# Unscaled rows to DRAM, norm factors applied after the fetch, and another order for the last tile and the last down projection

## The chip, the cores and the metric

One Trainium2 chip, one of its cores. The metric is the device time of one execution in microseconds (us); the kernel before takes 776.83 us, the median of three runs (776.01 to 776.99). PE is TensorE, ACT is ScalarE, DVE is VectorE, POOL is GpSimd, SP is SyncE; "SPq" and "ACTq" in a row are DMA issues by those engines' sequencers.

## The reference

One decoder layer for 512 tokens of width 1024, in float32. A mixing part (gated convolution and differential attention) ends in an output projection that is added to the residual. Then a mixture of 32 SwiGLU experts in 4 groups; each token goes to the best group and there to its best two experts. The part that matters here:

```python
h = h + mix @ w_out
hn2 = rms_norm(h, ffn_norm_g)            # h * rsqrt(mean(h*h) + eps) * g
logits_g = hn2 @ w_router_group          # [T, 4]
logits_e = hn2 @ w_router_expert         # [T, 32]
g_idx, g_gate = argmax, max of softmax(logits_g)
top-2 of the 8 logits of that group, softmax over the two -> exp_w
comb = one_hot(g_idx) * exp_w * g_gate   # [T, 32], two entries of a row are not zero
for each expert e:
    act = silu(hn2 @ w_gate[e]) * (hn2 @ w_up[e]) * comb[:, e]
    y  += act @ w_down[e]
h = h + y
```

## The kernel before

The 512 tokens are four tiles of 128 (c = 0 to 3), and `y` in SBUF holds the residual, 128 x 4 x 1024. Each expert gets up to 64 slots, two experts make a pair (q = 0 to 15), so that a pair fills the 128 partitions. An overflow loop at the end takes experts with more than 64 tokens; in the run shown it takes no trip.

The weights of the experts, 192 pieces of 1 MB, come in through a ring of 16 tiles (`we`) and one more (`wm`), all issued by SP at L726 in the order in which PE uses them. SP issues a piece when the tile that it goes into has been read for the last time, and at most eight DMAs are under way on its and ACT's queues together: each takes one of eight semaphores in turn and waits until the DMA that had it before has landed. 12 pieces are issued while the output projection runs, five more (`pump(RING + MORE)`) as the tiles that hold the projection's operands come free.

Between the output projection and the first expert stands a handover, once per token tile c:

- `out_rest` (L829) is the rest of the projection, `h_add` (L665) adds its half to `y` on DVE and squares it on ACT, `h_transposed` (L675) turns `y` on PE, and `router` (L685) multiplies it with the router's weights.
- `h_norm` (L744) is a generator of small DVE and ACT steps that makes `rstd`. Its last step multiplies `y[:, c]` by `rstd` and by the norm's gain (`gfb`, loaded at L657) into the tile `ht`, of which there is one, in a transposed element order, and writes `ht` to DRAM as `hrow` (L763, 512 KB, issued by ACT).
- `route` (L781) picks group and experts in 14 small DVE steps. `tail` (L814) interleaves `h_norm` and `route`, and for tile c - 1 it is emitted around the projection of tile c. Engines run their queues in order.
- `positions` and `place` count the tokens of each expert. Once tile 3 is placed, `prepare` (L926) makes the list of a pair's tokens (`one_hot`, `index`), and POOL fetches their rows from `hrow` with an indirect DMA (`fetch_rows`, L917, tile `xr`), after all four writes of `hrow` have landed. `gates` (L862) makes the weights `comb`, written to DRAM as `crow` and fetched per slot as `cw`.

Per pair, `turned` (L938) turns the fetched rows with eight PE transposes and copies them out of PSUM, four by ACT in one instruction and four by DVE in one. `gate_up` (L951), `activate` (L958), `down_t` (L964), `down` (L972), `down_split` (L982) and `combine` (L995) follow. `down` of the last pair makes both halves of the 1024 columns together; then `combine` is called for eight blocks of `y`, each with its DVE add (L1003) and its DMA to the output (L1140).

Of the kernel before, what the change touches and what calls it, by code (L numbers as in the profile page):

```python
# [17 lines left out]
P = 128  # L18
D = 1024
# [14 lines left out]
NONE = 2047  # L34
PAIRS = NE // 2
# [3 lines left out]
def layer(ctx: ExitStack, tc: tile.TileContext, x, attn_norm_g, w_in, conv_w, conv_out_g,  # L39
# [101 lines left out]
    G.dma_start(gst[19:27], ffn_norm_g.rearrange("o (k p) -> (o k) p", p=P))  # L141
    lt = ring.tile([P, 2, 2, HD], F32, name="lt", tag="w")
# [513 lines left out]
    gfb = po.tile([P, D], F32, name="gfb")  # L656
    A.dma_start(gfb, bass.AP(tensor=ffn_norm_g.tensor, offset=ffn_norm_g.offset, ap=[[0, P], [1, D]]))  # L657
# [37 lines left out]
    comb = kp.tile([P, NT, NE], F32, name="comb")  # L695
# [16 lines left out]
    def w_src(e, j):  # L712
# [5 lines left out]
        src = src.rearrange("(p k) f -> p k f", k=4)  # L718
        return src[:, 2 * (j - 4):2 * (j - 4) + 2], (2, 1024)
# [19 lines left out]
    crow = dram.tile([S, NE], F32, name="crow")  # L739
# [4 lines left out]
    def h_norm(c):  # L744
# [91 lines left out]
    for c in range(NT):  # L836
# [17 lines left out]
    advance(tails[3], 50)  # L854
# [7 lines left out]
    def gates():  # L862
        eg4 = rtt("eg4", NT, NG)
# [11 lines left out]
        V.reciprocal(gate, gate)  # L875
        w12 = rtt("w12", 2, NT)
# [6 lines left out]
        V.tensor_add(comb, oh1, oh2)  # L883
# [26 lines left out]
    def fetch(i, m):  # L910
        x = moe.tile([P, KD, P], F32, name="xr", tag="xr", bufs=2)
        w = moe.tile([P, NE], F32, name="cw", tag="cw", bufs=4)
        fetch_rows(x, i, m)
        return x, w

    def fetch_rows(x, i, m):
        G.indirect_dma_start(out=x[0:m].rearrange("p k q -> p (k q)"), out_offset=None, in_=hrow[:, :],  # L917
# [40 lines left out]
    def activate(act, p, h, w):  # L958
        t = moe.tile([P, FE], F32, name="sil", tag="sil")
        A.activation(t[HS[h]], p[HS[1 - h]], AF.Silu)  # L960
# [20 lines left out]

    def down_split(p, m):  # L982
        rh = moe.tile([P, 2, 512], F32R, name="rh", tag="rh", bufs=2)
        rl = moe.tile([P, 2, 512], F32R, name="rl", tag="rl", bufs=2)
        for hf in range(2):
            A.activation(rh[0:m, hf], p[hf][0:m], AF.Copy)  # L986
            V.tensor_sub(rl[0:m, hf], p[hf][0:m], rh[0:m, hf].bitcast(F32))  # L987
        return rh, rl
# [6 lines left out]
    def combine(parts, m, c, hf):  # L995
# [7 lines left out]
        V.tensor_add(ys, ys, p)  # L1003
# [20 lines left out]
    def overflow(inc):  # L1024

        n = nc.values_load(tot[0:1, 0:1], min_val=0, max_val=NE)
        with tc.For_i(0, n, 1):
# [25 lines left out]
            V.tensor_mul(le[0:SLOTS], le[0:SLOTS], cw[0:SLOTS])  # L1053
# [5 lines left out]
            activate(act, p, 0, wcol[0:SLOTS])  # L1059
# [7 lines left out]
    for _ in range(2):  # L1067
        G.memset(moe.tile([P, KD, P], F32, name="xr", tag="xr", bufs=2), 0.0)
    for _ in range(4):
        G.memset(moe.tile([P, NE], F32, name="cw", tag="cw", bufs=4), 0.0)  # L1070
    ready = prepare((0, 1), "S")()
    gates()
    xts = {0: turned(rows.pop(0), P, "K")}
    ready()
# [19 lines left out]
    def expert(e):  # L1094
# [6 lines left out]
        activate(acts[q], p, h, cws[q][HS[h], e:e + 1])  # L1101
# [72 lines left out]
```

## Time and profile before

| what | before |
|---|---|
| median of three runs | 776.83 us |
| the profiled execution | 779.3 us |
| its span, first to last instruction | 777.5 us |
| mean granted clock of PE, share of 2.4 GHz | 0.965 |
| busy: PE, DVE, ACT, POOL | 692.2, 308.8, 179.3, 73.3 us |
| moved by DMA | 230.19 MB |
| chain that ended last | PE 49%, DMA 34%, DVE 9%, ACT 4% |

The page of the profile gives the busy time of each engine and the chain of work that ended last. The chain is followed back from the last instruction, at each step to what released it. Busy PE is pipelined work and not PE at its peak. The other views are windows (busy times, the granted clock and the rate of DMA in a stretch), the timeline and the list of waits.

### The profile page before, as it was taken

To read this page: it belongs to the slowest core of one execution; us is meant where nothing else is said; L and a number is where in the kernel's file an instruction comes from. 1 tells how busy PE (TensorE), PEld (TensorE's weight loads), DVE (VectorE), ACT (ScalarE), POOL (GpSimd) and SP (SyncE) were. 2 spreads that over 40 slices of the span, in tenths; PEclk is the share of its full clock that TensorE was granted. 3 is DMA by queue.
4 is the path that set the end of the run, shared out by engine and by line. 5 is a ranking of instruction groups with operands and counts; after the bars stand their busy time and mean duration, and the time that the engine had idled before them with its cause. 6 is when DMAs were issued, how large, how long until landed. Compare 5 with 4: busy or idle time off the path is not lost.

```text
span 777.5 us, 8615 instructions
## 1 busy us (share of the span) xinstructions
PE 692.2 (89%) x3272; PEld 375.5 (48%) x3272; DVE 308.8 (40%) x593; ACT 179.3 (23%) x363; POOL 73.3 (9%) x100
## 2 busy tenths in 40 slices
PE   6998999999999409899999999999988988998985
PEld 5887787777777303334334334334334333333431
DVE  3565776687442641143224133223223123211243
ACT  3555545545242111010110110110110110110010
POOL 5020301021100120202002002002002001000000
PEclk9999999999999758899999999999999999999998
DMA  8231221111279745999999999999999999999942
GB/s 256 84 91 52 75 82 55 55 54 63 73 268 422 295 156 233 415 420 421 417 420 420 418 421 414 423 420 415 422 421 419 418 421 421 416 421 421 422 190 108
DMA packets 53418, 230.19 MB, mean 296 GB/s; under 512 B 6287, under 2 KB 20896, under 8 KB 28800
## 3 DMA queue, kind: packets, MB, share of 16 engines
q1 hardware_dynamic: 48848, 222.32, 71.2%
q0 software_dynamic: 3280, 4.63, 1.9%
q10 hardware_dynamic: 1248, 2.69, 0.9%
q8 instruction: 26, 0.43, 0.2%
q14 instruction: 16, 0.13, 0.0%
HBM read 229.67 MB, written 4.26 MB: 301 GB/s over the span
## 4 chain that ended last, share of the span: by engine, by line
PE 49%; DMA 34%; DVE 9%; ACT 4%; issue 2%; POOL 1%; SPq 0%; ACTq 0%; POOLq 0%; DVEq 0%
DMA we<-in_w_exp_up_dram 23%; PE pgu L955 11%; PE pdn L978 7%; PE pgu L956 3%; PE pcb L1000 3%; DMA wm<-in_w_exp_down_dram 3%; PE pq L117 3%; DMA we<-in_w_exp_down_dram 3%; PE pq L116 3%; PE pq L118 3%; DMA hrow<-ht 3%; PE pcb L1001 3%; DMA xr<-hrow,idx 2%; PE pcv L116 1%; PE pcv L118 1%
## 5 line engine op out<-in xcount | busy, mean ns | idle before, releaser
L956 PE MATMUL pgu<-we,xt 128*64 128x512 f32 x488 | 217.9, 598 | 14.5 <-DMA we<-in_w_exp_up_dram 14.5
L955 PE MATMUL pgu<-we,xt 128*64 128x512 f32 x480 | 214.8, 598 | 0.8 <-issue 0.8
L961 DVE SCALAR_TENSOR_TENSOR act<-sil,cw,pgu 64x512 f32<-64x512 f32 x32 | 35.9, 1121 | 220.7 <-ACT sil L960 220.7
L978 PE MATMUL pdn<-we,aT 128*64 128x512 f32 x480 | 118.7, 606 | 1.5 <-ACT aT L969 1.5
L955 PEld LDWEIGHTS pgu<-we,xt 128*64 128x64 f32 x480 | 64.2, 138 | 87.9 <-issue 85.8
L956 PEld LDWEIGHTS pgu<-we,xt 128*64 128x64 f32 x488 | 65.3, 138 | 68.9 <-issue 41.9
L960 ACT ACTIVATE sil<-pgu 64x512 f32<-64x512 f32 x32 | 18.9, 591 | 291.5 <-PE pgu L956 266.4
L978 PEld LDWEIGHTS pdn<-we,aT 128*64 128x64 f32 x480 | 36.5, 139 | 67.2 <-issue 62.4
L1000 PE MATMUL pcb<-rh,sel 128*128 128x512 f32 x128 | 55.5, 434 | 7.0 <-DVE y L1003 6.7
L987 DVE TENSOR_TENSOR rl<-pdn,rh 128x512 fp32r<-128x512 f32 x32 | 22.1, 692 | 94.5 <-ACT rh L986 94.5
L1003 DVE TENSOR_TENSOR y<-y,pcb 128x512 f32<-128x512 f32 x72 | 48.6, 687 | 17.2 <-PE pcb L1001 16.5
L1001 PE MATMUL pcb<-rl,sel 128*128 128x512 f32 x128 | 51.3, 400 | 0.3
L917 POOL DMA_INDIRECT xr<-hrow,idx x16 | 16.1, 1005 | 362.3 <-DVE vcol L907 335.8
L108 DVE TENSOR_TENSOR wlo<-raw,whi 128x1024 fp32r<-128x1024 f32 x30 | 37.7, 1256 | 22.3 <-ACT whi L101 22.3
L986 ACT ACTIVATE rh<-pdn 128x512 fp32r<-128x512 f32 x32 | 19.1, 597 | 112.4 <-PE pdn L978 112.4
L116 PE MATMUL pq<-whi,xh 128*128 128x512 f32 x96 | 41.0, 427 | 2.4 <-DVE st0h L353 1.6
L116 PE MATMUL pcv<-xh,whi 128*128 128x512 f32 x96 | 41.7, 435 | 0.0
L117 PE MATMUL pq<-wlo,xh 128*128 128x512 f32 x96 | 38.8, 404 | 0.5 <-DVE wlo L108 0.5
L118 PE MATMUL pq<-whi,xl 128*128 128x512 f32 x96 | 38.7, 403 | 0.0
L118 PE MATMUL pcv<-xh,wlo 128*128 128x512 f32 x96 | 38.0, 395 | 0.0
L117 PE MATMUL pcv<-xl,whi 128*128 128x512 f32 x96 | 37.8, 394 | 0.0
L1000 PEld LDWEIGHTS pcb<-rh,sel 128*128 128x128 f32 x128 | 24.4, 191 | 26.3 <-DVE y L1003 20.2
(227 smaller groups left out, 907.8 us busy)
## 6 DMA issues: line engine op xcount, KB each, us to landing
we<-in_w_exp_up_dram SPq DMA_DIRECT2D x61, 1024.0 KB, 19.8
we<-in_w_exp_gate_dram SPq DMA_DIRECT2D x60, 1024.0 KB, 19.8
we<-in_w_exp_down_dram SPq DMA_DIRECT2D x60, 1024.0 KB, 19.8
raw<-in_w_in_dram SPq DMA_DIRECT2D x24, 512.0 KB, 3.7
raw<-in_w_out_dram SPq DMA_DIRECT2D x8, 512.0 KB, 3.7
wm<-in_w_exp_gate_dram SPq DMA_DIRECT2D x4, 1024.0 KB, 19.8
wm<-in_w_exp_down_dram SPq DMA_DIRECT2D x4, 1024.0 KB, 19.8
wm<-in_w_exp_up_dram SPq DMA_DIRECT2D x3, 1024.0 KB, 16.4
```

Source lines behind the costliest of these rows:

```text
L108: V.tensor_sub(los[i], raws.pop(i), his[i].bitcast(F32))
L116: T.matmul(o, lh, rh, start=start, stop=False)
L117: T.matmul(o, lh, rl, start=False, stop=False)
L118: T.matmul(o, ll, rh, start=False, stop=stop)
L955: T.matmul(p[HS[1 - h]], l, w[2 * (k // 4)][:, k % 4], start=(k == 0), stop=(k == KD - 1))
L956: T.matmul(p[HS[h]], l, w[2 * (k // 4) + 1][:, k % 4], start=(k == 0), stop=(k == KD - 1))
L961: V.scalar_tensor_tensor(act[HS[h]].rearrange("s (c q) -> s q c", c=4), t[HS[h]].rearrange("s (q c) -> s q c", c=4), w, p[HS[h]].rearrange ...
L978: T.matmul(p[hf][HS[h]], aT[:, c, HS[h]], ws2[h][c // 2][:, c % 2, hf * 512:(hf + 1) * 512], start=(c == 0), stop=(c == 3))
L987: V.tensor_sub(rl[0:m, hf], p[hf][0:m], rh[0:m, hf].bitcast(F32))
L1000: T.matmul(p, s[0:m, ts], rh[0:m, hf], start=(n == 0), stop=False)
L1001: T.matmul(p, s[0:m, ts], rl[0:m, hf], start=False, stop=(n == last))
L1003: V.tensor_add(ys, ys, p)
```

## The change

The rows written to DRAM are `y` itself, in its own element order, issued right after `h_transposed(c, 1)`; the tile `ht`, the gain `gfb` and the large multiplication of `h_norm` are gone. `rstd` becomes column 32 of `comb`, so that it comes back with the gates; `activate` applies it as the scale of the Silu and `gate` is multiplied by it once more. The gain, loaded at the start as `gf` (one column per turned block), is applied where `turned` copies out of PSUM: ACT does so in four instructions, one per block, DVE in one. For the last tile all 14 routing steps come first and the norm's steps move into `gates`. The first two pairs are prepared one after the other and not together. In the last pair the down weights come by columns, each half of the columns is finished and split by itself, the selection matrix is made ahead of `combine_all`, and of the four blocks of a half one is added by ACT (copy) and POOL (add) in place of DVE.

```diff
+    gf = cons.tile([P, KD], F32, name="gf")
+    G.dma_start(gf, ffn_norm_g.rearrange("o (p k) -> (o p) k", k=KD))
-    gfb = po.tile([P, D], F32, name="gfb")
-    A.dma_start(gfb, bass.AP(tensor=ffn_norm_g.tensor, offset=ffn_norm_g.offset, ap=[[0, P], [1, D]]))
@@ w_src
+        if isinstance(e, int) and e >= NE - 2:
+            return src[:, :, 512 * (j - 4):512 * (j - 4) + 512], (4, 512)
@@ h_norm
-        t = po.tile([P, KD, P], F32, name="ht")
-        V.scalar_tensor_tensor(t, y[:, c].rearrange("p (q k) -> p k q", k=KD), n,
-                               gfb.rearrange("p (q k) -> p k q", k=KD), op0=OP.mult, op1=OP.mult)
-        A.dma_start(hrow[c * P:(c + 1) * P, :], t.rearrange("p k q -> p (k q)"))
+        V.tensor_copy(comb[:, c, NE:NE + 1], n)
@@ tail
+        if c == NT - 1:
+            for g in (gr, gn):
+                for _ in g:
+                    yield
+            return
@@ the loop over c, and after it
         h_transposed(c, 1)
+        A.dma_start(hrow[c * P:(c + 1) * P, :], y[:, c])
-    advance(tails[3], 50)
+    advance(tails[3], N_ROUTE)
@@ gates
+        advance(tails[3], 50)
+        V.tensor_mul(gate, gate, rstd)
@@ turned
+        x = x.rearrange("s (q k) -> s k q", k=KD)
-                V.tensor_copy(xt[:, 4 * k2:4 * k2 + 4, 0:m], p[:, :, 0:m])
+                ks = slice(4 * k2, 4 * k2 + 4)
+                V.tensor_tensor(xt[:, ks, 0:m], p[:, :, 0:m], bc(gf[:, ks, None], [P, 4, m]), op=OP.mult)
-                A.activation(xt[:, 4 * k2:4 * k2 + 4, 0:m], p[:, :, 0:m], AF.Copy)
+                for j in range(4):
+                    A.activation(xt[:, j, 0:m], p[:, j, 0:m], AF.Copy, scale=gf[:, j:j + 1])
@@ activate
-        A.activation(t[HS[h]], p[HS[1 - h]], AF.Silu)
+        A.activation(t[HS[h]], p[HS[1 - h]], AF.Silu, scale=r)
@@ down_cols (new)
+        p = bank("D", "pdn")
+        for c in range(4):
+            for h in range(2):
+                T.matmul(p[HS[h]], aT[:, c, HS[h]], ws2[h][:, c], start=(c == 0), stop=(c == 3))
@@ combine
-        V.tensor_add(ys, ys, p)
+        if to is None:
+            V.tensor_add(ys, ys, p)
+        else:
+            A.activation(to, p, AF.Copy)
+            G.tensor_tensor(ys, ys, to, op=OP.add)
@@ before the first expert
-    ready = prepare((0, 1), "S")()
+    ready = [prepare((q,), "S")() for q in range(2)]
@@ the last pair
-    down_pair(q, down_t(acts.pop(q), P))
-    for c in range(NT):
-        for hf in range(2):
-            combine([parts[q]], P, c, hf)
+    sel = select(vcol[:, q:q + 1], P)
+    combine_all((q - 1,))
+    aT = down_t(acts.pop(q), P)
+    r = split_tiles()
+    yt = moe.tile([P, 2, 512], F32, name="yt", tag="xr", bufs=2)
+    pd = [down_cols([wt.pop((2 * q + h, 4 + hf)) for h in range(2)], aT) for hf in range(2)]
+    for hf in range(2):
+        split_half(r, pd[hf], hf, P)
+        for c in (0, 1, 2, 3):
+            combine([(sel, *r)], P, c, hf, yt[:, hf] if c == 1 else None)
             nc.sync.dma_start(oc[:, c, 512 * hf:512 * hf + 512], y[:, c, 512 * hf:512 * hf + 512])
```

## Rows read from the trace of the kernel before

**Rows 1.** Windows: busy us (instructions) by engine, granted clock, DMA share, GB/s.

```profile
core 0: us, PE busy (x) PEld busy (x) DVE busy (x) ACT busy (x) POOL busy (x), PEclk, DMA share, GB/s
...
240.00:260.00 20.00, 18.39 (x97) 13.80 (x96) 8.80 (x36) 4.76 (x13) 0.61 (x2) 1.00 1.01 422
260.00:280.00 20.00, 3.56 (x20) 3.15 (x21) 13.07 (x45) 2.13 (x7) 2.03 (x6) 0.56 0.49 174
280.00:300.00 20.00, 8.96 (x45) 4.58 (x46) 5.99 (x28) 2.19 (x4) 4.14 (x4) 0.59 0.38 116
...
500.00:600.00 100.00, 91.41 (x422) 37.63 (x420) 28.65 (x45) 10.98 (x19) 7.99 (x8) 1.00 1.01 420
```

**Rows 2.** Chain that ended last: start us, us, what (a DMA: issue to landing).

```profile
252.60 7.66 DMA hrow<-ht
...
270.79 6.93 DMA hrow<-ht
277.83 2.05 DVE ht L761
...
286.12 4.53 DMA xr<-hrow,idx
...
312.45 8.56 DMA xr<-hrow,idx
...
711.79 0.64 PE pgu L956
```

**Rows 3.** Timeline of the handover: start us, us, engine, line [idle before <-releaser].

```profile
253.61 0.40 PE L118 MATMUL po<-w1h,ml 128*128 128x512 f32 x1
...
255.25 0.68 DVE L667 TENSOR_TENSOR y<-y,po 128x512 f32<-128x512 f32 x1
...
265.11 0.68 DVE L667 TENSOR_TENSOR y<-y,po 128x512 f32<-128x512 f32 x1
...
267.64 1.92 PE L688 MATMUL pr<-wrg,hT 128*128 128x36 f32 x8 [0.63 <-ACT hT L683]
...
279.80 0.18 DVE L778 TENSOR_REDUCE rm<-w 128x1 f32<-128x32 f32 x1
...
281.77 0.19 DVE L812 SCALAR_TENSOR_TENSOR posm<-ppos,ohm 128x32 f32<-128x32 f32 x1 [0.28 <-PE ppos L809]
...
283.58 0.16 DVE L906 TENSOR_SCALAR idx<-pi 128x1 int32<-128x1 f32 x1 [0.36 <-PE pi L904]
...
286.12 1.12 POOL L917 DMA_INDIRECT xr<-hrow,idx  x1 [24.09 <-DVE oh L882]
...
293.65 1.08 PE L955 MATMUL pgu<-we,xt 128*64 128x512 f32 x1 [0.82 <-issue]
```

**Rows 4.** Timeline of SP's queue: the first piece issued into a freed tile.

```profile
298.71 0.33 SPq L726 DMA_DIRECT2D we<-in_w_exp_up_dram  x1
```

**Rows 5.** List of waits, 300 to 745 us: us in total, times, longest.

```profile
PE pgu L956 <- DMA we<-in_w_exp_up_dram: 14.5, 12, 1.3
```

**Rows 6.** Groups of ACT by shape: count, busy us, mean ns, idle before.

```profile
L948 ACT ACTIVATE xt<-pxt 128x512 f32<-128x512 f32 x16 | 9.5, 593 | 9.4 <-PE pxt L944 9.4
...
L596 ACT ACTIVATE so<-pav,hc 128x128 f32<-128x128 f32 x16 | 5.8, 362 | 4.9 <-PE pav L592 4.8
```

**Rows 7.** Router weights' tile: ns min/median/max, first to last start us.

```profile
L148 POOL DMA_DIRECT2D wr<-in_w_router_expert_dram x1: 889/889/889, 10.9 to 10.9; - x1
L285 DVE TENSOR_TENSOR wrg<-wr,gT x1: 458/458/458, 37.5 to 37.5; 128x288 f32<-128x288 f32 x1
```

**Rows 8.** Timeline of the last pair, columns as in Rows 3.

```profile
754.94 0.48 DVE L992 TENSOR_SCALAR sel<-tokrow,vcol 128x512 fp32r<-128x512 f32 x1
755.48 7.09 PE L978 MATMUL pdn<-we,aT 128*64 128x512 f32 x32 [0.75 <-ACT aT L969]
...
763.85 5.91 DVE L1003 TENSOR_TENSOR y<-y,pcb 128x512 f32<-128x512 f32 x8
```

**Rows 9.** Groups of POOL: count, busy us, mean ns, idle before.

```profile
L428 POOL TENSOR_TENSOR cs<-cs,cz 128x512 f32<-128x512 f32 x4 | 5.1, 1283 | 63.7 <-DVE cs L426 63.7
```

More of the change, by code (lines that the diff above doesn't have):

```diff
@@ L34 @@
 NONE = 2047
+N_ROUTE = 14
 PAIRS = NE // 2
@@ L694, in layer @@
     kp = ctx.enter_context(tc.tile_pool(name="kp", bufs=1, side="right", reuse_waits="tile"))
-    comb = kp.tile([P, NT, NE], F32, name="comb")
+    comb = kp.tile([P, NT, NE + 1], F32, name="comb")
     posm = kp.tile([P, NT, NE], F32, name="posm")
@@ L738, in layer @@
     hrow = dram.tile([S, D], F32, name="hrow")
-    crow = dram.tile([S, NE], F32, name="crow")
+    crow = dram.tile([S, NE + 1], F32, name="crow")
     def rtt(name, *shape, dt=F32, bufs=1):
@@ L882, in gates @@
         V.tensor_mul(oh2, oh2, bc(w12[:, 1, :, None], [P, NT, NE]))
-        V.tensor_add(comb, oh1, oh2)
+        V.tensor_add(comb[:, :, 0:NE], oh1, oh2)
         A.dma_start(crow.rearrange("(c p) e -> p c e", p=P), comb)
@@ L910, in fetch @@
     def fetch(i, m):
-        x = moe.tile([P, KD, P], F32, name="xr", tag="xr", bufs=2)
-        w = moe.tile([P, NE], F32, name="cw", tag="cw", bufs=4)
+        x = moe.tile([P, D], F32, name="xr", tag="xr", bufs=2)
+        w = moe.tile([P, NE + 1], F32, name="cw", tag="cw", bufs=4)
         fetch_rows(x, i, m)
@@ L916, in fetch_rows @@
     def fetch_rows(x, i, m):
-        G.indirect_dma_start(out=x[0:m].rearrange("p k q -> p (k q)"), out_offset=None, in_=hrow[:, :],
+        G.indirect_dma_start(out=x[0:m], out_offset=None, in_=hrow[:, :],
                              in_offset=bass.IndirectOffsetOnAxis(ap=i[0:m, 0:1], axis=0),
@@ L980, in down, with down_cols, split_tiles, split_half @@
         return p
+    def down_cols(ws2, aT):
+        p = bank("D", "pdn")
+        for c in range(4):
+            for h in range(2):
+                T.matmul(p[HS[h]], aT[:, c, HS[h]], ws2[h][:, c], start=(c == 0), stop=(c == 3))
+        return p
+    def split_tiles():
+        return (moe.tile([P, 2, 512], F32R, name="rh", tag="rh", bufs=2),
+                moe.tile([P, 2, 512], F32R, name="rl", tag="rl", bufs=2))
+    def split_half(r, p, hf, m):
+        A.activation(r[0][0:m, hf], p[0:m], AF.Copy)
+        V.tensor_sub(r[1][0:m, hf], p[0:m], r[0][0:m, hf].bitcast(F32))
     def down_split(p, m):
-        rh = moe.tile([P, 2, 512], F32R, name="rh", tag="rh", bufs=2)
-        rl = moe.tile([P, 2, 512], F32R, name="rl", tag="rl", bufs=2)
+        r = split_tiles()
         for hf in range(2):
-            A.activation(rh[0:m, hf], p[hf][0:m], AF.Copy)
-            V.tensor_sub(rl[0:m, hf], p[hf][0:m], rh[0:m, hf].bitcast(F32))
-        return rh, rl
+            split_half(r, p[hf], hf, m)
+        return r
     def select(v, m):
@@ L993, in select, with combine @@
         return s
-    def combine(parts, m, c, hf):
+    def combine(parts, m, c, hf, to=None):
         p = bank("C", "pcb")
@@ L1052, in overflow @@
             wcol = lt_("wcol", 1)
-            V.tensor_mul(le[0:SLOTS], le[0:SLOTS], cw[0:SLOTS])
+            V.tensor_mul(le[0:SLOTS], le[0:SLOTS], cw[0:SLOTS, 0:NE])
             V.tensor_reduce(wcol[0:SLOTS], le[0:SLOTS], axis=AX.X, op=OP.add)
@@ L1058, in overflow @@
             act = moe.tile([P, FE], F32, name="act", tag="act", bufs=2)
-            activate(act, p, 0, wcol[0:SLOTS])
+            activate(act, p, 0, cw[0:SLOTS, NE:NE + 1], wcol[0:SLOTS])
             r = down_split(down([w[4:6]], down_t(act, SLOTS)), SLOTS)
@@ L1067, in layer @@
     for _ in range(2):
-        G.memset(moe.tile([P, KD, P], F32, name="xr", tag="xr", bufs=2), 0.0)
+        G.memset(moe.tile([P, D], F32, name="xr", tag="xr", bufs=2), 0.0)
     for _ in range(4):
-        G.memset(moe.tile([P, NE], F32, name="cw", tag="cw", bufs=4), 0.0)
-    ready = prepare((0, 1), "S")()
+        G.memset(moe.tile([P, NE + 1], F32, name="cw", tag="cw", bufs=4), 0.0)
+    ready = [prepare((q,), "S")() for q in range(2)]
     gates()
     xts = {0: turned(rows.pop(0), P, "K")}
-    ready()
+    for f in ready:
+        f()
     for cc in range(NT):
@@ L1100, in expert @@
         used(4)
-        activate(acts[q], p, h, cws[q][HS[h], e:e + 1])
+        activate(acts[q], p, h, cws[q][HS[h], NE:NE + 1], cws[q][HS[h], e:e + 1])
     def down_pair(q, aT):
```

5 lines of the change are left out of this document (2 added, 3 removed).

## The prediction

> **What bounds the kernel now.** I read the windows first [rows 1]. In the expert stage (500 to 600 us stands for all of 303 to 745) DMA is full, share 1.01 and 420 GB/s, while PE is busy 91 of 100 us: the stream of expert weights is the limit. From 240 to 260 us it is full as well (422 GB/s). Between, from 260 to 300 us, it is not: 174 and then 116 GB/s, that is 20 x 0.174 + 20 x 0.116 = 5.8 MB where 40 x 0.42 = 16.8 MB would have gone through. The ring is full of weights, no tile comes free before the first expert runs, and so some 26 us of the bound resource lie idle. PE runs there at a granted clock of 0.56 to 0.59, a mean of its two levels 1.2 and 2.4 GHz; before it, it was busy 18.4 of 20 us at 1.00.
>
> Second, the chain that ended last [rows 2]. From 250 to 286 us it alternates between the DVE instruction `ht` (2.05 to 2.21 us, four of them) and the landing of the write `hrow<-ht` (6.1 to 7.7 us): there is one `ht`, so the multiplication for tile c waits until the write of tile c - 1 has landed, and everything behind it on DVE waits too. The last write then lets the first fetch `xr` go, at 286.12. From 711.79 on the chain is PE's own work to the end; before that, every 60 us or so, it is a landing of weights.
>
> Third, the timeline [rows 3] for the order of events: `h_add` of tile 2 at 255.25, of tile 3 only at 265.11, its routing done at 281.77 (`posm`), token lists at 283.58, fetch at 286.12, first expert matmul at 293.65. SP gets its first free tile at 298.71, 5.06 us later [rows 4], and from there the stream runs without a gap. So what brings the first expert matmul forward by G brings the stream's restart and the end forward by G, as long as the stream stays the bound.
>
> Fourth, PE's waits for weights: 14.5 us in 12 waits over the expert stage [rows 5]. That is PE's reserve there, about 1 us per pair.
>
> **The change part by part. (1) `ht` and its wait are gone.** DVE loses four instructions of some 2.1 us and three waits of up to 3.40 us. I step through the queues with the old durations.
>
> - `h_add(2)`: PE issued the last projection matmul of tile 2 at 253.61 and could be answered 0.44 us later (the same distance as for tile 1), at 254.05. It came at 255.25 because DVE was behind [rows 3]. I take 254.05, a gain of 1.2 us.
> - `h_add(3)`: its matmuls follow `router(2)` on PE. For tile 2 `router` started 2.1 us after `h_add` and the next `h_add` was possible 2.6 us after that. 254.05 + 2.1 + 2.7 = 258.9 in place of 265.11.
> - `router(3)`: 258.9 + 2.1 = 261.0, and 1.1 us long at the full clock (1.92 at half [rows 3]), so 262.1. Then 0.5 us for `place(2)`.
> - Routing of tile 3: seven of its 14 steps, with `positions` and the start of `place`, stand between 279.80 and 281.77 [rows 3], which makes 0.25 us a step, 3.5 us for 14. The norm's steps no longer lie between them. With `positions` and `place` (0.5), one pair's `one_hot` (half of the old 1.2 us), `index` and the copy (0.5), the list of pair 0 stands at 262.6 + 3.5 + 0.5 + 0.6 + 0.5 = 267.7. With 0.45 us for POOL it could fetch at 268.2.
>
> **(2) The rows themselves.** ACT issues the write of tile 3 behind `hT(3)`, about 2.2 us after `h_add(3)`: 261.1. It lands 5.3 us later when DMA is quiet (the last one before, issued 279.91) and 7.66 us later beside the weights (252.60 in [rows 2]). This time it is beside the weights, so 268.8. POOL needed 0.87 us from the last landing to the fetch, so 269.6. Both paths end within 1.5 us; the rows are last. Bounds for the fetch: 268.2 (quiet write) to 270.5 (0.9 us worse than the slowest of four). DMAs added to ACT's queue: four, 0.33 us of issue each, as before.
>
> **(3) The fetch.** From issue to landing 4.53 us on quiet DMA (286.12) and 8.56 us beside the weights (312.45) [rows 2]. Which? The 5.8 MB of 260 to 300 us must still go through: at 420 GB/s they need 13.8 us, to 273.8 at most, and less the first fetches' own bytes (two of at most 0.5 MB) to 271.3 at least. The SP issues that waited for a write of `hrow` (8.4 us) or for `ht` (10.9 us) no longer do. So a fetch at 269.6 meets the stream for its first 2 to 3 us. I take 5.5 us, nearer to the quiet row: landing at 275.1. The Trainium skill (DMA: Bandwidth & Descriptors, Issuing engines are not separate DMA queues) says that DMAs from SP, ACT and POOL run on the same 16 engines and interleave; by that alone a fetch moved to 269.6 is a loaded one, 8.56 us, and the sum is 3 us smaller. The trace agrees with the page on the two prices; that the stream has run dry by about 272 is what I hold against it here.
>
> From landing to the first expert matmul it was 3.0 us (290.65 to 293.65). ACT's part of `turned` becomes four instructions; 128 x 128 with a per-partition factor costs 362 ns, the old one 593 [rows 6], so at most 1.45 in place of 0.59 us. It begins when the first four transposes are done, 1.1 us after landing, and ends at 2.6, ahead of DVE's half at 2.8. So 3.0 stays: 278.1, **G = 293.65 - 278.1 = 15.5 us**. Its bounds: fetch 268.2 with 4.53 gives 275.7 and G = 17.9; fetch 270.5 with 8.56 gives 282.1 and G = 11.6.
>
> **(4) Norm and gates moved behind the fetch.** `h_norm(3)` (2 us with two trips to ACT), one more multiplication and the gates (2.6 us) run on DVE from 268.5 to some 273.5, before the landing at 275.1 that DVE's copy in `turned` needs. `crow` lands about 275.5, `cw` by 280 (its first took 3 us). The Silu that now needs it comes 8.5 us after the first matmul. All hidden; without that cover, up to 2 us, inside the bounds above.
>
> **(5) Each pair.** 0.6 to 0.85 us more on ACT [rows 6], DVE's copy becomes a multiplication of the same size (an add of that size from PSUM takes 0.68 [rows 3], the copy 0.69). PE's reserve of 1 us per pair [rows 5] covers it even if all of it were on PE's path. Nothing.
>
> **(6) Start.** One more small DMA on POOL's queue, about 0.5 us for all behind it. The last of them, the router's weights, issued at 10.9 and landed at 18.8, is first used at 37.5 [rows 7]. Nothing.
>
> **(7) The last pair.** PE's chain from 711.79 on. The selection matrix, 0.48 us, ran at 754.94 beside PE; now it stands on DVE ahead of the adds on which PE waits: +0.46. Half 0 of the down projection is done after half of 7.09 us, so its split is hidden under half 1, and the first add comes at 763.1 in place of 763.85 [rows 8]: -0.75. Behind it DVE had eight adds in 5.91 us, PE filling one of two PSUM banks while DVE reads the other. Now it has six adds and the second split, but in c0, c2 the same bank follows itself (0.74 us from a freed bank to the next result), and the split of half 1 stands behind the adds of half 0: 7 x 0.69 + 2.0 of gaps = 6.85 us, +0.94. POOL's two adds (1.28 us each by the nearest row [rows 9]) end before DVE's last. Sum +0.65, the end of the adds at 770.4 in place of 769.8. Bounds: -0.7 (no gaps) to +1.3 (a POOL add last). The column pieces come 8 us or more before `down` needs them, except the last, 4 us.
>
> **The sum.** -15.5 + 0.65 = -14.85 us. The profiled execution took 779.3 us, 2.5 above the median; it would become 764.4, the median 776.83 - 14.85 = **761.98, say 762.0 us**.
>
> **Rivals.** *The fetch stays loaded* (the rule above; for it: every fetch in the expert stage; against: the bytes left): G = 11.6 to 12.5, 765 to 766.5.
>
> *The early writes hold back the adds.* `y` is one tile. If `h_add(c + 1)` had to wait until `hrow` has read `y[:, c]`, the wait for `ht` would return on `y`: `h_add(2)` at 259, `h_add(3)` at 268.4, the write at 270.6 landing at 277.6, fetch 278.4, landing 283, first matmul 286, G = 7.7, 769.8 us. Against it: in the last pair adds [rows 8] go on into other blocks of `y` while the block before is being written out. The change would then not do what it says.
>
> *PE becomes the bound* (slower). If `turned` and the Silu with their new factors cost PE more than its reserve, every pair pays. It decides from (14.5 + 14.85) / 15 = 2.0 us per pair on PE's path; at 3 us it gives 776.83 - 14.85 + 15 x 3 - 14.5 = 792.5 us. For it: ACT feeds every expert. Against: the price read is 0.85 at most, and ACT is a quarter busy.
>
> **How the numbers follow.** Forecast 0.73 (758.2 to 764.6 by its bounds), loaded fetch 0.17 (to 766.5), adds held back 0.04 (769.8), PE the bound 0.04, something else that eats the gain 0.02. Low is 776.83 - 17.9 - 0.7 = 758.2, rounded to 758; high is 766.5 and a little towards the third case, 768. A measurement can tell about 0.2% (1.6 us) from no change: faster 0.94, same 0.02, slower 0.04.
>
> **What the profile would show.** Right: no wait of DVE for `hrow`; `h_add(3)` near 259; the first `xr` at 268 to 270.5, landing at 273 to 278; the first expert matmul near 278 and SP's first freed tile 5 us after; idle DMA between 260 and 300 us shrunk from 26 to about 11 us; PE's last wait for weights near 696; from there to the last add 0.6 us longer than the old 58. Wrong: `h_add` waiting for `hrow`; a fetch of 8 us or more; gaps in the stream after the restart; more PE time per pair than 29 to 30 us; the adds of the last pair in another order than I stepped through.

## The result, and the profile after

The changed kernel takes **767.14 us** (median of four runs, 766.17 to 768.06), the kernel before beside it 776.42 us: a ratio of 0.9884 (95% interval 0.9863 to 0.9906), 9.3 us faster. Forecast were 762.0 us, between 758 and 768. The profiled execution took 767.56 us, its span 765.8 us; forecast were 764.4 us for it.

Windows of the changed kernel, columns and stretches as in [rows 1]:

```profile
260.00:280.00 20.00, 5.20 (x43) 4.38 (x45) 11.35 (x58) 4.45 (x12) 4.71 (x9) 0.58 0.83 331
280.00:300.00 20.00, 20.00 (x94) 7.22 (x94) 4.25 (x8) 2.51 (x6) 1.76 (x2) 0.91 0.70 275
500.00:600.00 100.00, 91.42 (x422) 39.47 (x420) 27.79 (x45) 12.58 (x27) 7.98 (x8) 1.00 1.01 419
```

The expert stage is as it was: DMA full, 419 GB/s, PE 91.4 of 100 us. Between 260 and 300 us DMA now moves 20 x 0.331 + 20 x 0.275 = 12.1 MB in place of 5.8.

Timeline of the changed kernel's handover, columns as in [rows 3] (SPq and ACTq are DMA issues; a row with x2 runs to the end of its second issue):

```profile
259.22 6.39 SPq L729 DMA_DIRECT2D we<-in_w_exp_down_dram  x2
...
259.64 0.68 DVE L668 TENSOR_TENSOR y<-y,po 128x512 f32<-128x512 f32 x1
...
261.07 0.33 ACTq L851 DMA_DIRECT2D hrow<-y  x1
...
267.42 0.19 DVE L812 SCALAR_TENSOR_TENSOR posm<-ppos,ohm 128x32 f32<-128x32 f32 x1 [0.28 <-PE ppos L809]
...
268.76 0.16 DVE L914 TENSOR_SCALAR idx<-pi 128x1 int32<-128x1 f32 x1 [0.36 <-PE pi L912]
...
270.97 1.12 POOL L925 DMA_INDIRECT xr<-hrow,idx  x1 [9.40 <-DVE hv L753]
...
276.94 1.94 PE L953 MATMUL pxt<-idf,xr 128*128 128x128 f32 x8 [7.03 <-DMA xr<-hrow,idx]
...
279.81 1.08 PE L966 MATMUL pgu<-we,xt 128*64 128x512 f32 x1 [0.82 <-ACT xt L959]
...
285.33 0.33 SPq L729 DMA_DIRECT2D we<-in_w_exp_up_dram  x1
```

The chain that ended last, for the same stretch (start us, us, what; a DMA from issue to landing):

```profile
270.97 5.84 DMA xr<-hrow,idx
...
276.94 1.10 PE pxt L953 x4
...
278.07 1.15 ACT xt L959 x4
```

Against [rows 2 to 4]: no DVE instruction waits for `hrow` any more; `h_add(3)` begins at 259.64 in place of 265.11, the last `posm` at 267.42 in place of 281.77, the first fetch at 270.97 in place of 286.12, the first expert matmul at 279.81 in place of 293.65 (13.84 us earlier), and the first freed tile is refilled at 285.33 in place of 298.71 (13.38 us earlier).

PE's wait for weights in the expert stage, from the list of waits, as in [rows 5]:

```profile
PE pgu L967 <- DMA we<-in_w_exp_up_dram: 13.7, 12, 1.3
```

The last pair, rows of the timeline as in [rows 8]:

```profile
742.57 7.09 PE L999 MATMUL pdn<-we,aT 128*64 128x512 f32 x32 [0.75 <-ACT aT L981]
...
751.09 7.03 SPq L1175 DMA_DIRECT2D out_dram<-y  x8
...
755.50 1.28 POOL L1033 TENSOR_TENSOR y<-y,yt 128x512 f32<-128x512 f32 x1 [2.65 <-ACT yt L1032]
755.87 1.28 DVE L1030 TENSOR_TENSOR y<-y,pcb 128x512 f32<-128x512 f32 x2 [0.82 <-PE pcb L1027]
```

From the first `pdn` to the last add's end it is 14.6 us (742.57 to 757.15); before it was 14.3 (755.48 to 769.76). The last output is issued at 757.72.

So 13.4 us were gained at the restart of the stream, and the median shows 9.3. The experiments ask where the rest went, and what each part of the change is worth.

### The profile page after: what moved, and what is told of

The parts are those of the page before. It is cut to its first block, busy times and chain, and to the rows that moved or that the text cites. A ratio compares the mean times of both kernels' runs of the same rounds, so it can differ in the third digit from the quotient of the medians.

```text
span 765.8 us, 8682 instructions
## 1 busy us (share of the span) xinstructions
PE 690.6 (90%) x3272; PEld 379.6 (50%) x3272; DVE 300.9 (39%) x593; ACT 192.4 (25%) x413; POOL 76.4 (10%) x103
## 4 chain that ended last, share of the span: by engine, by line
PE 52%; DMA 29%; DVE 9%; ACT 5%; issue 2%; POOL 1%; SPq 0%; DVEq 0%; POOLq 0%; ACTq 0%
DMA we<-in_w_exp_up_dram 18%; PE pgu L966 13%; PE pdn L990 7%; DMA we<-in_w_exp_down_dram 6%; PE pgu L967 4%; DMA wm<-in_w_exp_down_dram 3%; PE pq L118 3%; PE pq L119 3%; PE pq L117 3%; PE pcb L1026 2%; DMA xr<-hrow,idx 2%; PE pcb L1027 2%; PE pcv L117 1%; PE pcv L119 1%; PE pcv L118 1%
## 5 line engine op out<-in xcount | busy, mean ns | idle before, releaser
L967 PE MATMUL pgu<-we,xt 128*64 128x512 f32 x488 | 218.4, 599 | 13.7 <-DMA we<-in_w_exp_up_dram 13.7
L990 PE MATMUL pdn<-we,aT 128*64 128x512 f32 x448 | 109.4, 598 | 0.8 <-ACT aT L981 0.8
L972 ACT ACTIVATE sil<-pgu,cw 64x512 f32<-64x512 f32 x32 | 21.9, 683 | 289.5 <-PE pgu L967 264.7
```

What stands on the lines that cost most here:

```text
L967: T.matmul(p[HS[h]], l, w[2 * (k // 4) + 1][:, k % 4], start=(k == 0), stop=(k == KD - 1))
L990: T.matmul(p[hf][HS[h]], aT[:, c, HS[h]], ws2[h][c // 2][:, c % 2, hf * 512:(hf + 1) * 512], start=(c == 0), stop=(c == 3))
```

## The experiments

Times read from the profiled executions (us), medians from all runs of the kernel. "Start" is DVE's addition `h_add` of tile 0, which lies ahead of everything that the kernels do differently in the handover; "write" is the issue of the last `hrow` write, "fetch" that of the first `xr`, "matmul" the first expert matmul, "refill" SP's issue into the first freed tile, "stream" the time from there to the issue of the last output.

| kernel | median | start | write | fetch | matmul | refill | stream |
|---|---|---|---|---|---|---|---|
| before | 776.42 | 244.63 | 279.91 | 286.12 | 293.65 | 298.71 | 471.1 |
| x1 before, again | 776.68 | 244.25 | 276.61 | 282.89 | 290.49 | 296.81 | 469.9 |
| x4 order alone | 779.77 | 244.11 | 280.79 | 287.34 | 294.59 | 300.25 | 471.2 |
| x3 two `ht` | 772.18 | 243.35 | 270.44 | 276.65 | 284.03 | 289.16 | 471.0 |
| x5 rows alone | 766.76 | 245.46 | 261.16 | 271.46 | 280.34 | 285.67 | 471.0 |
| x2 old last pair | 765.89 | 245.18 | 260.88 | 270.56 | 279.71 | 285.04 | 471.3 |
| after | 767.14 | 245.38 | 261.07 | 270.97 | 279.81 | 285.33 | 472.4 |
| x12 after, again | 766.67 | 245.77 | 261.46 | 271.50 | 280.64 | 285.92 | 472.3 |
| x6 plain turn | 766.84 | 244.71 | 260.40 | 270.19 | 279.34 | 284.36 | 472.2 |
| x7 quiet fetch | 765.78 | 244.44 | 260.14 | 270.63 | 277.75 | 283.25 | 472.4 |
| x8 idle matmuls | 763.92 | 244.08 | 259.77 | 269.83 | 277.59 | 281.24 | 471.8 |
| x9 last pair in order | 765.82 | 245.01 | 260.70 | 270.77 | 279.62 | 284.78 | 470.8 |
| x10 x7, x8 and x9 | 764.08 | 245.02 | 260.71 | 270.74 | 277.83 | 281.48 | 471.5 |
| x11 x8 and x2 | 763.02 | 244.65 | 260.35 | 270.37 | 278.42 | 283.73 | 471.3 |

The last column is the first finding: "refill" moves over 19 us, from 281.24 to 300.25, and "stream" stays within 469.9 to 472.4. What is gained before the refill arrives at the end.

A profiled execution is one of its kernel's times and need not be the typical one: x3's took 770.02 us and x8's 762.86, 2.2 and 1.1 below their medians, while those of x4 (781.25), x11 (765.06) and x12 (768.15) lie 1.5 to 2.0 above. The rows show where a step stands; what it is worth is read from the medians.

### x1: the kernel before, once more

> The kernel before, unchanged, profiled once more. Theory 1 (the shown execution of before was a long one: 779.3 us where its median is 776.4, and some 2.4 us of what the prediction missed lie there): this execution takes 775.5 to 777.5 us, and the difference to the first one is spread over the span as a granted clock below full speed, not one event between 240 and 300 us. Theory 2 (the execution shown was ordinary and profiling adds those 2.5 us every time): 779 us again.

Measured: 776.68 us median, this execution 776.57; ratio to before 1.0003 (0.9992 to 1.0014). The chain that ended last, and below it two timeline rows of SP and DVE in the same stretch:

```profile
267.24 2.13 DVE ht L761
269.40 5.01 DMA hrow<-ht
274.52 2.05 DVE ht L761
...
282.89 4.59 DMA xr<-hrow,idx
...
290.49 1.09 PE pgu L955
```

```profile
266.66 0.33 SPq L726 DMA_DIRECT2D we<-in_w_exp_down_dram  x1
...
267.24 2.13 DVE L761 SCALAR_TENSOR_TENSOR ht<-y,rstd,gfb 128x1024 f32<-128x1024 f32 x1
```

Theory 1 holds in its time and in the main falls in its place: of the 2.7 us between the two executions 1.9 stand at the refill (298.71 against 296.81), and 1.0 lies at the end, where it is the clock. The first part comes from the landings of two writes. The write of tile 1, issued at 262.17, had landed by 266.66, where SP issues the piece that takes its semaphore over: 4.5 us at most, where the execution of [rows 2] had 6.1, and `ht` at 267.24 has no wait. The write of tile 2 takes 5.01 us where [rows 2] show 6.93. The first expert matmul comes at 290.49, **3.2 us earlier than in the execution from which the forecast was made** (0.4 of it an earlier start), and the median belongs to this execution rather than to that one. From the matmul to the refill it is 6.32 us here and 5.06 there, so that 1.9 us are left of the 3.2: PE was at 1.2 GHz until 295.9 here, 5.4 us into the first expert, and until 296.5 there, 2.9 us into it. Against this execution the change brings the first expert matmul forward by 10.7 us, not 13.8, and the refill by 11.5, not 13.4.

The second part lies in the combine ahead of the last `pdn`. Windows of the execution before, and below it of this one at the same place, columns as in [rows 1]:

```profile
750.00:754.00 4.00, 3.82 (x10) 2.27 (x9) 2.65 (x5) 0.00 (x0) 0.00 (x0) 0.57 0.01 6
```

```profile
748.00:752.00 4.00, 3.32 (x13) 1.68 (x12) 3.55 (x7) 0.21 (x1) 0.00 (x0) 1.00 0.02 6
```

There PE fell to 1.2 GHz from 750.5 to 753.9; here it did not. From PE's last wait for weights to the first `pdn` it is 43.7 us there (711.79 to 755.48) and 42.7 here.

### x3: two buffers

```diff
...
-        t = po.tile([P, KD, P], F32, name="ht")
+        t = po.tile([P, KD, P], F32, name="ht", bufs=2)
...
```

> Before, with two buffers ht in place of one. For room the gain vector is not loaded; in the multiplication a weight tile of the same size stands in for it, so the rows hold other values and only the time is read. Theory 1 (two causes: the wait for the one buffer, and the write that comes only after the norm): the wait goes, the write of tile 3 is issued at 267 to 268 us in place of 279.9, the first expert matmul comes 8 to 9 us earlier, 767 to 768.5 us. Theory 2 (the buffer alone was the cause): all of the 13.8 us, 762.5 to 763.5 us. Theory 3 (only where the write starts from matters): within 1.6 us of before.

Measured: 772.18 us, ratio 0.9952 (0.9938 to 0.9965). The chain:

```profile
262.68 2.11 DVE ht L759
268.36 2.05 DVE ht L759
...
276.65 4.38 DMA xr<-hrow,idx
...
284.03 1.09 PE pgu L953
```

The wait for the buffer is gone, and that alone is worth 4.5 us. No theory had that time. My 8 to 9 were counted from 293.65, from which it is 9.6; from x1's 290.49 to 284.03 it is 6.5 us, 0.9 of it an earlier start, and this execution is 2.2 us shorter than its median. The write still has to wait for norm and routing of tile 3 and for `ht` itself (268.36 to 270.41), and is issued 9.4 us later than the unscaled one (270.44 against 261.07). The fetch then finds DMA quieter: 4.38 us.

### x4: the order alone

```diff
+        if c == NT - 1:
+            for g in (gr, gn):
+                for _ in g:
+                    yield
+            return
...
-    advance(tails[3], 50)
+    advance(tails[3], 14)
     positions(NT - 1)
     place(NT - 1)
+    advance(tails[3], 50)
...
-    ready = prepare((0, 1), "S")()
+    ready = [prepare((q,), "S")() for q in range(2)]
...
```

> Before, with the order alone: for tile 3 the routing runs ahead of the norm, and the list of pair 0 is made alone, ahead of that of pair 1; ht, its one buffer and the scaled write stay. Theory 1 (the rows bound the first fetch, the lists did not): the last write still lands at about 285 us, the fetch is issued at most 0.5 us earlier, 775.5 to 776.5 us. Theory 2 (the lists bounded it as much): 4 us or more faster, below 772.5 us.

Measured: 779.77 us, ratio 1.0040 (1.0027 to 1.0054): **slower** by 3.1 us, which neither theory had. Timeline of DVE:

```profile
269.51 2.05 DVE L761 SCALAR_TENSOR_TENSOR ht<-y,rstd,gfb 128x1024 f32<-128x1024 f32 x1 [2.49 <-DMA hrow<-ht]
...
277.17 0.19 DVE L812 SCALAR_TENSOR_TENSOR posm<-ppos,ohm 128x32 f32<-128x32 f32 x1 [0.28 <-PE ppos L809]
...
278.70 2.06 DVE L761 SCALAR_TENSOR_TENSOR ht<-y,rstd,gfb 128x1024 f32<-128x1024 f32 x1
```

The last `ht` begins at 278.70 without a wait: its buffer is free by then, and what holds it is the norm, which now stands behind the routing. In x1 it began at 274.52, straight behind the landing. While the write carries the norm, routing first is the wrong order; it is right only once the rows don't wait for the norm. A second part is the write of tile 1, for which `ht` at 269.51 waits 2.49 us; it was issued at 261.86, behind two weight pieces at 259.71 and 260.13, where x1 has one. How the 3.1 us divide between the two was not separated.

### x5 and x2: the rows alone, and with the order

x5 takes the order and the new last pair out of the changed kernel; x2 takes out the last pair only.

```diff
...
-    aT = down_t(acts.pop(q), P)
-    r = split_tiles()
...
+    down_pair(q, down_t(acts.pop(q), P))
+    for c in range(NT):
+        for hf in range(2):
+            combine([parts[q]], P, c, hf)
```

> The changed kernel with the unscaled rows alone: norm and routing of tile 3 interleaved again, both lists of the first two pairs made together, the last pair as before. Theory 1 (the unscaled rows carry nearly all; the order is worth 1 to 2 us because the write lands only at 270, and the new last pair costs 1.6 us): the first fetch at 272 to 273 us, 766.5 to 768 us, level with the changed kernel. Theory 2 (the order carries a good part of the gain): fetch at 275 us or later, over 770 us.

> The changed kernel with the last pair as it was before (selection matrix made behind the second-last combine, down weights by rows, eight adds on DVE, output in order of DVE's adds). Theory 1 (from PE's last wait for weights to the last output DMA's issue the new last pair takes 1.64 us longer): 765.5 us, 1.6 us faster than the changed kernel; the last output is issued some 58 us after PE's last wait for weights. Theory 2 (columns and POOL's two adds do what they look made for, and the 1.64 us are the clock or the difference between two executions): 767.1 us or more.

Measured: x5 766.76 us (ratio 0.9872, 0.9857 to 0.9887), x2 765.89 us (0.9862, 0.9844 to 0.9881). The unscaled rows alone bring 9.9 of the 10.5 us that x2 has: theory 1 of x5 in its time. In x5 both lists are ready at 269.5 (`idx` at 269.38 and 269.53) and the write lands at 270.45, so that the rows are last there too. The order is worth less than the 1 to 2 us of that theory: 0.9 us lie between the two medians, whose intervals overlap, and 0.35 between the two executions, from start to first expert matmul. x2 fits theory 1. Timeline of its last pair:

```profile
742.06 7.09 PE L988 MATMUL pdn<-we,aT 128*64 128x512 f32 x32 [0.75 <-ACT aT L979]
...
750.44 5.90 DVE L1028 TENSOR_TENSOR y<-y,pcb 128x512 f32<-128x512 f32 x8
751.14 5.55 SPq L1169 DMA_DIRECT2D out_dram<-y  x8
```

The last output is issued at 756.36, 14.30 us behind the first `pdn`; in the changed kernel it was 757.72 - 742.57 = 15.15. "Stream" is 471.3 in place of 472.4. The medians differ by 1.25 us, but their intervals overlap: on medians alone it would not be told.

### x6: a plain turn

```diff
-                V.tensor_tensor(xt[:, ks, 0:m], p[:, :, 0:m], bc(gf[:, ks, None], [P, 4, m]), op=OP.mult)
+                V.tensor_copy(xt[:, ks, 0:m], p[:, :, 0:m])
-                for j in range(4):
-                    A.activation(xt[:, j, 0:m], p[:, j, 0:m], AF.Copy, scale=gf[:, j:j + 1])
+                A.activation(xt[:, 0:4, 0:m], p[:, :, 0:m], AF.Copy)
```

> The changed kernel with the gain factors left out of the copies behind the transposes: ACT has one instruction there in place of four, DVE a copy in place of a multiplication. Theory 1 (each pair's extra work lies beside PE, within its reserve): 766.5 to 767.7 us, no change, and PE's busy time per 100 us stays 91. Theory 2 (ACT's four instructions hold PE up in every pair): 16 pairs times the 0.45 us by which four instructions (1.14 us) are longer than one (0.69 us) are 7 us, and 760 us.

Measured: 766.84 us, ratio 0.9881 (0.9862 to 0.9900), against 0.9884 for the changed kernel. Theory 1. PE waits 13.1 us for weights in 12 waits, against 13.7. The gain factors in every pair cost nothing that the median shows, and PE did not become the bound. The Silu's factor was not taken out by itself.

### x7: two weight pieces out of the fetch's way

```diff
...
-    pump(RING + MORE)
+    pump(RING + MORE - 2)
...
     xts = {0: turned(rows.pop(0), P, "K")}
+    issuer[0] = A
+    pump(RING + MORE)
+    issuer[0] = nc.sync
```

> The changed kernel with the last two of the 17 early weight pieces (1 MB each) issued by ACT behind the first four transposes, so that the write of tile 3 and the first fetch meet fewer weights. Theory 1 (the write's 8.88 us and the fetch's 5.84 us are the weights beside them; quiet they were 5.3 and 4.5 us): the write lands by 268, the fetch 4.5 us after its issue at about 269, the first expert matmul 2 to 3 us earlier, but the 2 MB still have to pass, 4.8 us at 420 GB/s, in the time in which DMA idles, so that the end comes 2 to 3 us earlier: 764 to 765 us. Theory 2 (the bytes moved behind the fetch are missing later): first matmul earlier, end not: 767 us.

Measured: 765.78 us, ratio 0.9866 (0.9847 to 0.9886). The chain:

```profile
260.14 9.47 DMA hrow<-y
...
270.63 4.12 DMA xr<-hrow,idx
...
277.75 1.08 PE pgu L968
```

The fetch takes 4.12 us in place of 5.84 (6.14 in x12), so the two pieces were its price. The write is no shorter: issued 260.14, landed 269.61, 9.5 us. The pieces taken away were issued at 265 in the changed kernel, behind the write, so that they were not what it met. That it was the pieces ahead of it was not tested. Refill comes 2.1 us earlier, 0.9 of it an earlier start; the median is 1.4 us lower, between the two theories (764 to 765, and 767), and the intervals overlap.

### x8: idle matmuls

```diff
+    pd_ = bank("T", "pdum")
+    for _ in range(15):
+        T.matmul(pd_, onesb, tokrow[:, 0:256].bitcast(BF), start=True, stop=True)
     gates()
     xts = {0: turned(rows.pop(0), P, "K")}
```

> The changed kernel with 15 matmuls of 512 columns, whose result nobody reads, on PE between the token lists and the first fetch's landing, where PE waits. It leaves nothing out. Theory 1 (after its idle time PE runs at half clock until 283.6 us, so the first transposes and the first half of the first expert take about twice their time): at full clock the transposes take 1.1 in place of 1.94 us and the first expert is 3 to 4 us earlier through; SP's first freed tile comes 1 us earlier and the later ones up to 4 us: 763 to 766 us. Theory 2 (only the first freed tile sets the stream): 766 us. Theory 3 (the stream has its own pace, PE's clock does not matter): 767 us.

Measured: **763.92 us**, ratio 0.9848 (0.9826 to 0.9871), 3.2 us below the changed kernel. Windows, columns as in [rows 1]:

```profile
276.00:278.00 2.00, 1.16 (x12) 0.87 (x13) 0.79 (x2) 1.14 (x4) 0.60 (x1) 1.00 0.00 0
278.00:280.00 2.00, 2.00 (x12) 0.86 (x10) 0.00 (x0) 0.00 (x0) 1.40 (x2) 1.00 0.04 5
280.00:282.00 2.00, 2.00 (x12) 0.78 (x10) 0.00 (x0) 0.00 (x0) 0.00 (x0) 1.00 0.07 5
```

The changed kernel in the same place:

```profile
276.00:278.00 2.00, 1.06 (x5) 1.09 (x6) 0.00 (x0) 0.00 (x0) 0.00 (x0) 0.50 0.26 64
...
282.00:284.00 2.00, 2.00 (x8) 0.68 (x6) 0.00 (x0) 0.00 (x0) 0.00 (x0) 0.60 0.00 0
```

With the idle matmuls the clock is at 1.00 (2.4 GHz) throughout; the changed kernel has 0.50 (1.2 GHz) there and full speed only from 283.6 on. The eight transposes take 1.14 us in place of 1.94, and from the first expert matmul to the refill it is 3.65 us in place of 5.52. Theory 1: PE's half clock between the fetch's landing and the refill costs 2.7 us (0.8 in the transposes, 1.9 in the first expert), against 3.2 in the medians. The refill itself comes 4.1 us earlier, but 1.3 of that is this execution's earlier start. The intervals of the two kernels still overlap by a little; x11 repeats the comparison.

### x9: the last pair in another order

```diff
...
+        if q == PAIRS - 1:
+            sel = select(vcol[:, q:q + 1], P)
         expert(2 * q + 1)
...
+            combine([(sel, *r)], P, c, hf, yt[:, hf] if c == 1 else None, "CCGG"[c])
+            if c == 1 and hf == 0:
+                split_half(r, pd[1], 1, P)
+        for c in (0, 2, 3, 1):
```

> The changed kernel with its last pair put in another order: the selection matrix is made before the last expert, so that it does not stand ahead of the adds; the four blocks of a half take the PSUM tags C, C, G, G in place of C four times; the split of half 1 stands behind the second of half 0's adds; the outputs are issued as their adds end (c = 0, 2, 3, 1). Theory 1 (the new last pair's 1.64 us are the order: 0.6 us for the selection matrix, the rest for banks and for outputs that wait in SP's queue behind POOL's add): about 2.5 us faster than the changed kernel, 764 to 765.5 us, below the 765.9 us of the changed kernel with the old last pair. Theory 2 (DVE's adds from PSUM, 0.7 us each, set the end in any order, and POOL's add of 1.28 us the last one): no faster than with the old last pair, 765.5 to 767.5 us.

Measured: 765.82 us, ratio 0.9866 (0.9843 to 0.9890): Theory 2's time, level with the old last pair. Timeline:

```profile
741.58 7.09 PE L999 MATMUL pdn<-we,aT 128*64 128x512 f32 x32 [0.75 <-ACT aT L981]
...
750.08 6.01 SPq L1179 DMA_DIRECT2D out_dram<-y  x8
...
753.39 1.28 DVE L1030 TENSOR_TENSOR y<-y,pgu 128x512 f32<-128x512 f32 x2
753.42 1.27 POOL L1033 TENSOR_TENSOR y<-y,yt 128x512 f32<-128x512 f32 x1 [1.59 <-ACT yt L1032]
```

The adds do end earlier, 13.1 us behind the first `pdn` in place of 14.6. But seven outputs are then issued within 3.3 us (752.30 to 755.58), the last of them 0.9 us behind the last add, and the span ends 9.1 us after that issue, where it was 8.1 in the changed kernel and 8.3 in x2. From the first `pdn` to the end of the span it is 23.1 us, as in the changed kernel (23.2); x2 has 22.6. What x9 gains lies ahead of `pdn`: without the selection matrix before the adds, `pdn` comes 0.5 us sooner behind PE's last wait for weights (44.0 us against 44.5). That the seven transfers wait for each other fits this, but no run shows it.

### x10 and x11: together

The edits are those shown for x7, x8 and x9 (x10), and for x8 and x2 (x11).

> The last-pair order of x9, the two late weight pieces of x7 and the 15 idle matmuls of x8 together. If the three places are independent, their gains add up: x7 gave 1.4 and x8 gave 3.2 us on the changed kernel; with 2.5 us from the last pair 760 us, with nothing from it 762.5 us. If the quieter fetch lands before the idle matmuls have ended (they ran from 268.5 to 274.5 us, the quiet fetch landed at 274.75), x7's part is lost: 761.5 to 764 us.

Measured: 764.08 us, ratio 0.9848 (0.9826 to 0.9871), no faster than x8 and at the upper end of the third case. The fetch landed at 274.80 but the idle matmuls ran until 276.0, so the transposes came at 275.86 and the first expert matmul at 277.83; counted from the start that is 0.7 us sooner than in x8, where x7 gained 1.1 on the changed kernel. And ACT issued the two late pieces at 276.66 and 277.14; by an estimate from 420 GB/s their 2 MB need 5 us, until about 281.7, when the first tile comes free (281.48). Which of the two spends the gain, no run separates.

> The changed kernel with the 15 idle matmuls of x8 and the last pair as it was before. If the two places are independent, their gains add: 767.1 - 3.2 - 1.25 = 762.7 us, range 761.5 to 763.5, and faster than both kernels. If the old last pair gained only from its own execution's luck, 764 us as x8. The stream starts again when the first tile comes free, some 4 us after the first expert matmul, as in x8 (3.65 us), and PE's first expert matmul to the last output's issue takes about 476 us.

Measured: **763.02 us**, ratio 0.9826 (0.9810 to 0.9842), on one chip with x12 at 0.9877 (0.9859 to 0.9895): 3.65 us below the changed kernel and 13.5 below the kernel before, the lowest median of all. Its profiled execution was its slowest, 765.06 us (the others took 761.74 to 763.05). Its windows:

```profile
276.00:278.00 2.00, 1.22 (x12) 1.14 (x12) 0.47 (x1) 0.92 (x4) 0.00 (x0) 1.00 0.09 21
278.00:280.00 2.00, 1.58 (x4) 0.58 (x6) 0.32 (x2) 0.23 (x1) 1.55 (x2) 0.59 0.06 3
```

Here the clock fell again. The idle matmuls ended at 275.35 and the transposes at 276.37 still ran at full speed, but in the 0.83 us in which PE then waited for ACT, the clock went to its half, and the refill came 5.31 us after the first expert matmul, where some 4 were expected and x8 had 3.65. In x8 the same gaps (1.02 and 0.84 us) left it at full speed. So the idle matmuls help in some executions and not in others, which fits the spread of 3.3 us between this kernel's five times; what decides it stays open.

### x12: the changed kernel, once more

> The changed kernel, unchanged, profiled once more beside x11 on the same chip. If what is read from its first execution holds: 766.2 to 768.1 us; the fetch 9 to 10 us after the issue of tile 3's write; 5.3 to 5.6 us from the first expert matmul to the first freed tile; 15.1 us from the first down matmul of the last pair to the last output's issue, where before took 14.3. If these were chance, they fall elsewhere: the write in 8 us or less, the last pair in 14.5 or less.

Measured: 766.67 us median, 768.15 in this execution. The chain, and below it the last pair's rows of the timeline:

```profile
271.50 6.14 DMA xr<-hrow,idx
...
280.64 1.09 PE pgu L966
```

```profile
743.10 7.09 PE L999 MATMUL pdn<-we,aT 128*64 128x512 f32 x32 [0.75 <-ACT aT L981]
...
751.61 7.02 SPq L1175 DMA_DIRECT2D out_dram<-y  x8
```

All four readings hold: the write took 9.0 us (261.46 to 270.49), the fetch came 10.0 us after its issue, the refill 5.28 us after the first expert matmul, and the last output was issued at 758.24, 15.14 us behind the first `pdn`. They belong to the kernel, not to one execution.

## Why the prediction was right, and where it was off

The direction, the place and the mechanism were right, the gain was not: 14.85 us forecast, 9.3 measured. Of the 5.6 us missed, 3.2 lie in the terms: the profiled execution, whose own forecast was 764.4, took that much longer. Another 2 us lie in the step from that execution to the median, and 0.4 in the median of the kernel before (776.42 in place of 776.83).

- **The bound** (stream of weights): right. "Stream" in the table is the same within 2.5 us over fourteen executions, and 13.4 us at the refill are 13.7 at PE's last wait for weights (711.79 in [rows 2], 698.08 after).
- **The wait for `ht`** (step 1): right. From `h_add(0)` to `h_add(3)` the sum gave 14.27 us (244.63 to 258.9), the trace has 14.26. x3 shows that the buffer alone is worth 4.5 us; the rest of what the rows bring, 5.4 us (772.18 to x5's 766.76, both with the old last pair), is the write that no longer waits for norm, routing and `ht`.
- **The write** (step 2): mis-sized by 1.2 us. 7.66 us were taken, 8.88 measured, 9.02 in x12. One row of the kernel before stood for "beside the weights", and that is not one price: the four writes of the changed kernel, all beside the weights, took 7.87, 5.79, 8.98 and 8.88 us. What sets it stays open; the two pieces behind the write do not (x7). The rows were last, as forecast, and the lists (`idx` at 268.76) 1.2 us ahead of the landing.
- **The fetch** (step 3): 5.5 us taken, 5.84 measured. The size was right, the reason only half. The step let SP wait for the writes no longer. It does: each DMA takes over a semaphore whose last DMA has to have landed, and SP's piece at 265.29 went out when the write of tile 2 had landed at 265.21, 6.1 us behind the piece before it (the row 259.22, x2). So DMA had not run dry by 272: the last of the 17 pieces landed at 276.5. The fetch met two pieces, which landed at 273.69 and 276.49, and x7 without them has 4.12. The loaded price of 8.56 [rows 2] belongs to a stream with its whole queue behind it: here the first fetch took 5.6 to 6.1 us beside the two pieces, and one in the full stream 7.8 to 8.8. The Trainium skill (DMA: Bandwidth & Descriptors, Issuing engines are not separate DMA queues) says that DMAs of different issuers interleave on the same 16 engines. x7 agrees: POOL's fetch is 1.7 us shorter without SP's two pieces beside it.
- **From landing to matmul**: 3.0 us forecast, 3.0 measured (276.81 to 279.81), with ACT's four instructions in 1.14 us. The refill then came 5.52 us after the matmul where 5.06 was taken [rows 4]: PE ran at 1.2 GHz until 283.6, 3.8 us into the first expert, where before it was 2.9 (until 296.5). A later clock was not in the sum: +0.46.
- **Norm and gates behind the fetch** (step 4), **each pair** (step 5): right, nothing (DVE is done with both at 274.5, the fetch lands at 276.8; x6).
- **Start** (step 6): nothing was taken; it is about 0.45 us. From the multiplication of the router's weights ([rows 7], 37.5) to `h_add(0)` it is 207.0 to 207.1 us in the three executions that begin as before with `ht` in one buffer, and 207.5 in nine of ten that begin as the changed kernel. Which of the new instructions it is was not tested. (x3 and x8 both have some 1.5 us less, and the same distance between them. That is the clock: every other execution has PE at 1.2 GHz once, at about 67 to 71 or 198 to 202 us, and these two do not; the difference arises in that stretch.)
- **The last pair** (step 7): +0.65 taken; from PE's last wait for weights to the last output it grew from 58.0 to 59.6 us (59.5 in x12, 58.3 in x2), so +1.2 to +1.6. The adds were right: 14.5 us forecast from the first `pdn` to the end of the last add, 14.6 measured. So was the selection matrix, +0.46: from PE's last wait to `pdn` it is 44.5 us, and 44.0 in x9, which makes the matrix sooner. Before it was 43.7; the other 0.3 us stand in x2 as well (44.0) and belong to some other part of the change, which was not tested. One term was not in the sum. SP issues in order: the outputs of c = 2 and 3 stand behind POOL's add of c = 1, which ends at 756.78, and go out at 757.25 and 757.72, 0.57 us behind the last add, where before the last one went out with it.

For the profiled execution the terms add up: first matmul +1.7 (write 1.2, from its landing to the fetch 0.15, fetch 0.35), refill +0.46, last pair +1.0, in sum 3.2. That `h_add(0)` came 0.75 us later than in the execution before is made up by the write's issue, 0.8 us closer behind it than counted.

**The step that missed most** is the last one, "the median 776.83 - 14.85". G was counted against one execution, whose first expert matmul came at 293.65, and then taken from the median. That execution and its median were 2.5 us apart, and I did not ask where in the span these lay. Beside x1, whose time is the median's, 1.9 us of them stand at the refill, and the larger part of that, the landings of two writes, is in the very chain that the change removes; 1.0 us is the clock in the last combine. Counted from x1, the refill comes 11.5 us earlier (296.81 to 285.33), and the stream with the last pair takes 2.5 us longer (469.9 to 472.4, of which 1.0 is that x1's clock did not fall): 9.0 us, as the two executions differ (776.57 and 767.56), and 9.3 in the medians. G by the first expert matmul would be 10.7; it is the refill that counts.

Of the rivals, the loaded fetch did not come (5.84), the adds were not held back by the writes of `y` (`h_add(3)` at 259.64), and PE did not become the bound (13.7 us of waits left).

## What to carry to other kernels

Before a gain is taken from a median, profile the old kernel twice: here a chain of DMA landings differed by 2.8 us between two executions, and the gain of removing it is what the typical execution spends there. Compare the two where the bound resource starts again, and look at the granted clock of every stretch, which differed too. Take work off the path before reordering what is left: routing ahead of the norm made the kernel 3.1 us slower while the write carried the norm (a longer write of tile 1 is part of it), and gained 0.9 us, not clear of noise, once it didn't. Where a stage hands over to a full stream, look at the clock of the first instructions behind the idle time: here they ran at 1.2 GHz, and their time was part of the path.

## What the runs showed of the hardware

- 15 matmuls that nobody reads, in PE's idle time, brought 3.2 us on the changed kernel (x8) and 2.9 us on the one with the old last pair (x11 against x2), though in the profiled execution of x11 the clock fell to 1.2 GHz in a wait of 0.83 us behind them, and in x8 it did not.
- Where PE's clock falls differs from one execution to the next: two of fourteen (x3, x8) keep 2.4 GHz up to 263 us, worth 1.5 us, and three (x1, x8, x10) keep it in the last combine, worth 1.0 us.
- The same kernel's write of 512 KB from the same place in the queue took 6.93 us in one execution [rows 2] and 5.01 in another (x1).
- A write of 512 KB beside the weights took 5.8 to 9.0 us in the changed kernel, that of tile 3 8.7 to 9.5 over its runs (x2 and x7 are the ends); taking away the pieces issued behind it did not shorten it (x7).
